# Three PSUM tiles, one load across two halves and a second store: a change to a batch-norm-ReLU kernel

## Chip, cores, metric

The kernel runs on one core of a Trainium2 chip. The metric is the device time of one execution in microseconds (us); lower is better.

## What is computed

```python
# x: (32, 128, 32, 32) float32; gamma, beta, running_mean, running_var: (128,)
normalized = (x - running_mean[None, :, None, None]) / np.sqrt(running_var[None, :, None, None] + eps)
scaled = normalized * gamma[None, :, None, None] + beta[None, :, None, None]
return np.maximum(scaled, 0).astype(np.float32)
```

With scale = gamma / sqrt(var + eps) and bias = beta - mean * scale, this is one ReLU(scale * x + bias) per row of 1024 numbers. 16.78 MB go in and 16.78 MB come out, and nothing is used twice.

## The kernel before

The 4096 rows (batch times channel) are laid out as two halves of 128 partitions x 16 rows. A partition's 16 rows lie next to each other in memory (64 KB), so a transfer of n rows is 128 runs of n x 4 KB. SyncE issues the loads, ScalarE runs the ReLUs in place and issues the stores, and a small chain of TensorE, ScalarE and VectorE makes scale and bias.

```python
TILES = ((0, 0, 2), (0, 2, 4), (0, 4, 8), (0, 8, 16), (1, 0, 16))   # half, first row, end

LOAD_CUTS = {(1, 8)}
STORE_CUTS = {(0, 1)}

HALVES = {(1, 0), (1, 1)}
# ... (cut: signature; P = 128, J = 16, HW = 1024, Q = 8)
    tiles = []
    for t, a, b in TILES:
        xt = data.tile([P, b - a, HW], F32, name=f"x{t}_{a}")
        cuts = [a] + [j for j in range(a + 1, b) if (t, j) in LOAD_CUTS] + [b]
        for c, d in zip(cuts, cuts[1:]):
            nc.sync.dma_start(out=xt[:, c - a : d - a, :], in_=xr[t, :, c:d, :])
        tiles.append((t, a, b, xt))

    raw = params.tile([Q, 4, J], F32, name="raw")
    for k, src in enumerate((running_var, gamma, running_mean, beta)):
        nc.scalar.dma_start(out=raw[:, k, :], in_=src.rearrange("(q j) -> q j", j=J))
    # ... (cut: eps_t, and rep, the 8 x 128 matrix that copies 8 partitions to 128)
    cols = psum.tile([P, 4, J], F32, name="cols")

    for a, b in ((0, 2), (2, 3), (3, 4)):
        nc.tensor.matmul(
            cols[:, a:b, :].rearrange("p k j -> p (k j)"),
            rep.rearrange("q r s -> q (r s)"),
            raw[:, a:b, :].rearrange("q k j -> q (k j)"),
            start=True,
            stop=True,
        )
    std_t = params.tile([P, J], F32, name="std_t")
    nc.scalar.activation(out=std_t, in_=cols[:, 0, :], func=ACTF.Sqrt, bias=eps_t[:, 0:1], scale=1.0)
    rstd_t = params.tile([P, J], F32, name="rstd_t")
    nc.vector.reciprocal(out=rstd_t, in_=std_t)
    scale_t = params.tile([P, J], F32, name="scale_t")
    nc.vector.tensor_mul(out=scale_t, in0=cols[:, 1, :], in1=rstd_t)
    ms_t = params.tile([P, J], F32, name="ms_t")
    nc.vector.tensor_mul(out=ms_t, in0=cols[:, 2, :], in1=scale_t)
    bias_t = params.tile([P, J], F32, name="bias_t")
    nc.vector.tensor_sub(out=bias_t, in0=cols[:, 3, :], in1=ms_t)

    with tc.manual_schedule(engines={mybir.EngineType.Activation}):
        for t, a, b, xt in tiles:
            first = a
            for j in range(a, b):
                step = HW // 2 if (t, j) in HALVES else HW
                for w in range(0, HW, step):
                    nc.scalar.activation(
                        out=xt[:, j - a, w : w + step],
                        in_=xt[:, j - a, w : w + step],
                        func=ACTF.Relu,
                        bias=bias_t[:, j : j + 1],
                        scale=scale_t[:, j : j + 1],
                    )
                if j + 1 == b or (t, j + 1) in STORE_CUTS:
                    nc.scalar.dma_start(
                        out=outr[t, :, first : j + 1, :], in_=xt[:, first - a : j + 1 - a, :]
                    )
                    first = j + 1
```

## Time and profile before

| what | value | from |
|---|---|---|
| time | 83.55 us, median of 3 (83.50 to 83.62) | timing |
| span of the profiled run | 81.7 us | page |
| ScalarE busy | 39.1 us, 48% | engine row |
| first load issued, first data packet | 0.81, 1.8 us | timeline, packet records |
| first ReLU, first store issued | 9.44, 10.71 us | timeline |
| last load landed, last store issued | 46.8, 55.95 us | timeline |
| DMA rate, 46.4 to 60.8 us | 435 GB/s | DMA view |

The lines behind this table stand in the prediction. In the timeline a line is: start, duration, engine (ACTq and SPq are the issuing sequencers of ScalarE and SyncE), source line, operation, and in brackets how long the engine was idle before and what ended that. In the DMA view each line of a queue gives packets, MB, and the time of its packets as a share of 16 engines' time. Three more lines are needed for comparison, the waits of the kernel before (in total, times, longest):

```profile
ACT x L105 <- DMA x<-in_x_dram: 7.7, 3, 3.6
...
ACT std_t L89 <- PE cols L81: 4.2, 1, 4.2
...
ACT x L105 <- DVE bias_t L97: 1.0, 1, 1.0
```

ScalarE waits for loads three times, 3.6 us at most; it waits for the last of the matmuls before its square root.

### The profile page before, as it was taken

Reading aid. Unit: us, or ns where it says so; the run is one execution under the profiler, and the core shown is the slowest. Engines: PE = TensorE matmul, PEld = TensorE weight load, DVE = VectorE, ACT = ScalarE, POOL = GpSimd, SP = SyncE. Lnnn points to the kernel's source line nnn. Section 1 sums busy time; section 2 is a strip of 40 time slices with the busy share of each in tenths; the row PEclk is TensorE's granted clock in tenths of the full one; section 3 lists DMA queues with packets and bytes.
Section 4 is the critical chain, followed back from the end, with each engine's and each line's share of the span. In section 5 each row is a group of like instructions: output and inputs, shape, how many; then the busy total and the mean of one; then the engine's idle time right before and its main releaser. Section 6 shows DMA issues by size and latency. Waiting matters only on the chain.

```text
span 81.7 us, 128 instructions
## 1 busy us (share of the span) xinstructions
PE 1.7 (2%) x6; PEld 1.5 (2%) x6; DVE 0.8 (1%) x5; ACT 39.1 (48%) x36; POOL 0.8 (1%) x6
## 2 busy tenths in 40 slices
PE   0008000000000000000000000000000000000000
PEld 0007000000000000000000000000000000000000
DVE  0000300000000000000000000000000000000000
ACT  0600477799039999199997199993000000000000
POOL 3000000000000000000000000000000000000000
DMA  2899999989899898969789699996991999998290
GB/s 44 313 422 481 409 481 417 497 369 497 369 385 481 375 491 357 541 293 605 321 373 589 273 489 393 513 497 273 513 770 64 449 513 513 513 513 385 128 513 0
DMA packets 1793, 33.56 MB, mean 411 GB/s; under 512 B 257, under 2 KB 257, under 8 KB 513
## 3 DMA queue, kind: packets, MB, share of 16 engines
q1 hardware_dynamic: 864, 16.78, 48.6%
q10 hardware_dynamic: 928, 16.78, 47.8%
q14 instruction: 1, 0.00, 0.0%
HBM read 16.78 MB, written 16.78 MB: 411 GB/s over the span
## 4 chain that ended last, share of the span: by engine, by line
DMA 56%; ACT 10%; issue 2%; SPq 0%
DMA x<-in_x_dram 56%; ACT x L105 10%; SPq L56 0%
## 5 line engine op out<-in xcount | busy, mean ns | idle before, releaser
L105 ACT ACTIVATE x<-x,bias_t,scale_t 128x1024 f32<-128x1024 f32 (+1 forms) x34 | 37.5, 1178 | 10.0 <-DMA x<-in_x_dram 7.7
L89 ACT ACT_TABLE_LOAD x1 | 1.3, 1283 | 2.7 <-issue 2.7
L89 ACT ACTIVATE std_t<-cols,eps_t 128x16 f32<-128x16 f32 x1 | 0.3, 276 | 4.2 <-PE cols L81 4.2
L81 PE MATMUL cols<-raw,rep 8*128 8x16 f32 (+1 forms) x6 | 1.7, 384 | 6.4 <-DMA raw<-in_gamma_dram 6.3
L81 PEld LDWEIGHTS cols<-raw,rep 8*128 8x128 f32 x6 | 1.5, 307 | 6.5 <-issue 6.3
L68 POOL TENSOR_SCALAR_AFFINE_SELECT rep<-rep 8x128 f32<-8x128 f32 x1 | 0.4, 394 | 0.1
L91 DVE RECIPROCAL rstd_t<-std_t 128x16 f32<-128x16 f32 x1 | 0.3, 253 | 7.5 <-ACT std_t L89 7.5
L67 POOL MEMSET rep<- 8x128 f32 x1 | 0.2, 195 | 0.3 <-POOLq L133 0.3
L93 DVE TENSOR_TENSOR scale_t<-cols,rstd_t 128x16 f32<-128x16 f32 x1 | 0.2, 174 | 0.1
L95 DVE TENSOR_TENSOR ms_t<-cols,scale_t 128x16 f32<-128x16 f32 x1 | 0.2, 174 | 0.0
L97 DVE TENSOR_TENSOR bias_t<-cols,ms_t 128x16 f32<-128x16 f32 x1 | 0.2, 174 | 0.0
L133 POOL MEMSET const-bfloat16-1.0<- 128x1 bf16 x1 | 0.1, 108 | 0.0
L133 POOL MEMSET const-float32-0.0<- 128x1 f32 x1 | 0.1, 105 | 0.3 <-issue 0.3
L133 POOL MEMSET const-uint8-127<- 128x1 uint8 x1 | 0.1, 107 | 0.0
L133 POOL MEMSET const-float32-1.0<- 128x1 f32 x1 | 0.1, 105 | 0.0
L65 DVE MEMSET eps_t<- 128x1 f32 x1 | 0.1, 59 | 0.9 <-PEq L133 0.9
## 6 DMA issues: line engine op xcount, KB each, us to landing
x<-in_x_dram SPq DMA_DIRECT2D x3, 4096.0 KB, 38.6
out_dram<-x ACTq DMA_DIRECT2D x1, 4096.0 KB, 28.6
x<-in_x_dram SPq DMA_DIRECT2D x2, 1024.0 KB, 5.8
x<-in_x_dram SPq DMA_DIRECT2D x1, 2048.0 KB, 11.3
out_dram<-x ACTq DMA_DIRECT2D x1, 2048.0 KB
out_dram<-x ACTq DMA_DIRECT2D x2, 512.0 KB, 19.1
out_dram<-x ACTq DMA_DIRECT2D x1, 1024.0 KB
raw<-in_running_var_dram ACTq DMA_DIRECT2D x1, 0.5 KB
```

What stands on the lines that cost most here:

```text
L65: nc.vector.memset(eps_t, float(eps))
L67: nc.gpsimd.memset(rep, 1.0)
L68: nc.gpsimd.affine_select(out=rep, in_=rep, compare_op=mybir.AluOpType.is_equal, fill=0.0, base=0, pattern=[[0, P // Q], [-1, Q]], channel ...
L81: nc.tensor.matmul(cols[:, a:b, :].rearrange("p k j -> p (k j)"), rep.rearrange("q r s -> q (r s)"), raw[:, a:b, :].rearrange("q k j -> q ...
L89: nc.scalar.activation(out=std_t, in_=cols[:, 0, :], func=ACTF.Sqrt, bias=eps_t[:, 0:1], scale=1.0)
L91: nc.vector.reciprocal(out=rstd_t, in_=std_t)
L93: nc.vector.tensor_mul(out=scale_t, in0=cols[:, 1, :], in1=rstd_t)
L95: nc.vector.tensor_mul(out=ms_t, in0=cols[:, 2, :], in1=scale_t)
L97: nc.vector.tensor_sub(out=bias_t, in0=cols[:, 3, :], in1=ms_t)
L105: nc.scalar.activation(out=xt[:, j - a, w : w + step], in_=xt[:, j - a, w : w + step], func=ACTF.Relu, bias=bias_t[:, j : j + 1], scale=sc ...
L133: nc = _bacc.Bacc("TRN2", target_bir_lowering=False, num_devices=1)
```

## The change

It does three things. The parameters get three tiles in PSUM (the memory into which TensorE writes the matmuls' results) and in SBUF (the one that holds the tiles of x) in place of one (variance and gamma share the first), so that a reader need not wait for matmuls that it does not use. Rows 8 to 15 of the first half and 0 to 7 of the second come in one 8 MB transfer, with a hand-built access pattern that jumps from half to half in each partition. Rows 8 to 15 of the second half get a tile of their own, and so the second half goes out in two stores of 4 MB in place of one of 8 MB. One ReLU fewer is cut in two.

```diff
-TILES = ((0, 0, 2), (0, 2, 4), (0, 4, 8), (0, 8, 16), (1, 0, 16))
-LOAD_CUTS = {(1, 8)}
+TILES = (((0, 0, 2),), ((0, 2, 4),), ((0, 4, 8),), ((0, 8, 16), (1, 0, 8)), ((1, 8, 16),))
-HALVES = {(1, 0), (1, 1)}
+HALVES = {(1, 0)}
 ...
+            (t0, a, b), (t1, c, _) = pieces
+            pitch = ((t1 - t0) * P * J + c - a) * HW
+            nc.sync.dma_start(
+                out=xt,
+                in_=bass.AP(tensor=xr.tensor, offset=xr[t0, :, a:b, :].offset,
+                    ap=[[J * HW, P], [pitch, 2], [HW, b - a], [1, HW]]))
+        for i, (t, a, b) in enumerate(pieces):
+            tiles.append((t, a, b, xt[:, i]))
 ...
-    raw = params.tile([Q, 4, J], F32, name="raw")
+    for a, srcs in ((0, (running_var, gamma)), (2, (running_mean,)), (3, (beta,))):
+        raw[a] = params.tile([Q, len(srcs), J], F32, name=f"raw{a}")
 ...
-    cols = psum.tile([P, 4, J], F32, name="cols")
+    cols = []
     for a, b in ((0, 2), (2, 3), (3, 4)):
+        c = psum.tile([P, b - a, J], F32, name=f"cols{a}")
 ...
```

(Cut: the branch for single pieces and the readers of the three tiles, which follow from this. Some lines are joined.)

More of the change, by code (lines that the diff above doesn't have):

```diff
@@ L51 @@
     tiles = []
-    for t, a, b in TILES:
-        xt = data.tile([P, b - a, HW], F32, name=f"x{t}_{a}")
-        cuts = [a] + [j for j in range(a + 1, b) if (t, j) in LOAD_CUTS] + [b]
-        for c, d in zip(cuts, cuts[1:]):
-            nc.sync.dma_start(out=xt[:, c - a : d - a, :], in_=xr[t, :, c:d, :])
-        tiles.append((t, a, b, xt))
-    raw = params.tile([Q, 4, J], F32, name="raw")
-    for k, src in enumerate((running_var, gamma, running_mean, beta)):
-        nc.scalar.dma_start(out=raw[:, k, :], in_=src.rearrange("(q j) -> q j", j=J))
+    for pieces in TILES:
+        n = len(pieces)
+        rows = pieces[0][2] - pieces[0][1]
+        xt = data.tile([P, n, rows, HW], F32, name=f"x{pieces[0][0]}_{pieces[0][1]}")
+        if n == 1:
+            ((t, a, b),) = pieces
+            nc.sync.dma_start(out=xt[:, 0], in_=xr[t, :, a:b, :])
+        else:
+            (t0, a, b), (t1, c, _) = pieces
+            pitch = ((t1 - t0) * P * J + c - a) * HW
+            nc.sync.dma_start(
+                out=xt,
+                in_=bass.AP(
+                    tensor=xr.tensor,
+                    offset=xr[t0, :, a:b, :].offset,
+                    ap=[[J * HW, P], [pitch, 2], [HW, b - a], [1, HW]],
+                ),
+            )
+        for i, (t, a, b) in enumerate(pieces):
+            tiles.append((t, a, b, xt[:, i]))
+    raw = {}
+    for a, srcs in ((0, (running_var, gamma)), (2, (running_mean,)), (3, (beta,))):
+        raw[a] = params.tile([Q, len(srcs), J], F32, name=f"raw{a}")
+        for k, src in enumerate(srcs):
+            nc.scalar.dma_start(out=raw[a][:, k, :], in_=src.rearrange("(q j) -> q j", j=J))
     eps_t = params.tile([P, 1], F32, name="eps_t")
@@ L76 @@
     )
-    cols = psum.tile([P, 4, J], F32, name="cols")
+    cols = []
     for a, b in ((0, 2), (2, 3), (3, 4)):
+        c = psum.tile([P, b - a, J], F32, name=f"cols{a}")
         nc.tensor.matmul(
-            cols[:, a:b, :].rearrange("p k j -> p (k j)"),
+            c.rearrange("p k j -> p (k j)"),
             rep.rearrange("q r s -> q (r s)"),
-            raw[:, a:b, :].rearrange("q k j -> q (k j)"),
+            raw[a].rearrange("q k j -> q (k j)"),
             start=True,
@@ L87 @@
         )
+        cols.append(c)
     std_t = params.tile([P, J], F32, name="std_t")
-    nc.scalar.activation(out=std_t, in_=cols[:, 0, :], func=ACTF.Sqrt, bias=eps_t[:, 0:1], scale=1.0)
+    nc.scalar.activation(
+        out=std_t, in_=cols[0][:, 0, :], func=ACTF.Sqrt, bias=eps_t[:, 0:1], scale=1.0
+    )
     rstd_t = params.tile([P, J], F32, name="rstd_t")
@@ L92 @@
     scale_t = params.tile([P, J], F32, name="scale_t")
-    nc.vector.tensor_mul(out=scale_t, in0=cols[:, 1, :], in1=rstd_t)
+    nc.vector.tensor_mul(out=scale_t, in0=cols[0][:, 1, :], in1=rstd_t)
     ms_t = params.tile([P, J], F32, name="ms_t")
-    nc.vector.tensor_mul(out=ms_t, in0=cols[:, 2, :], in1=scale_t)
+    nc.vector.tensor_mul(out=ms_t, in0=cols[1][:, 0, :], in1=scale_t)
     bias_t = params.tile([P, J], F32, name="bias_t")
-    nc.vector.tensor_sub(out=bias_t, in0=cols[:, 3, :], in1=ms_t)
+    nc.vector.tensor_sub(out=bias_t, in0=cols[2][:, 0, :], in1=ms_t)
     with tc.manual_schedule(engines={mybir.EngineType.Activation}):
```

## The prediction

> **What bounds the kernel now.** I read the page first: the busy row of the engines, then the DMA lines, then the chain that ended last.
>
> ```profile
> span 81.7 us, 128 instructions
> PE 1.7 (2%) x6; PEld 1.5 (2%) x6; DVE 0.8 (1%) x5; ACT 39.1 (48%) x36; POOL 0.8 (1%) x6
> ...
> HBM read 16.78 MB, written 16.78 MB: 411 GB/s over the span
> ## 4 chain that ended last, share of the span: by engine, by line
> DMA 56%; ACT 10%; issue 2%; SPq 0%
> ```
>
> No compute engine is busy for more than 48% of the span, and the chain runs mostly through loads. The chain as printed stops with ScalarE at 55.9 us, though the span is 81.7, so its last third is no instruction at all: it must be the stores draining. I checked that with the DMA view over three stretches: loads alone with the parameters, loads mixed with stores, stores alone. The first line of each is its packet count and rate, the following ones its queues (q1 carries the loads, q10 the stores and parameters).
>
> ```profile
> DMA packets 456, 4.13 MB, mean 409 GB/s; under 512 B 80, under 2 KB 80, under 8 KB 80
> ...
> DMA packets 868, 14.71 MB, mean 429 GB/s; under 512 B 98, under 2 KB 98, under 8 KB 354
> ## 3 DMA queue, kind: packets, MB, share of 16 engines
> q1 hardware_dynamic: 448, 12.58, 85.5%
> q10 hardware_dynamic: 420, 2.13, 14.9%
> ...
> DMA packets 284, 6.26 MB, mean 435 GB/s; under 512 B 30, under 2 KB 30, under 8 KB 30
> ```
>
> These are 2 to 12.1 us, 12.1 to 46.4 us and 46.4 to 60.8 us. The rate never leaves 409 to 435 GB/s, and the shares of the two queues in the middle stretch add to 100.4%: all 16 DMA engines are full from about 2 us until the end. (The 40-slice row seems to show holes late in the span, slices of 64 GB/s. A packet is counted in the slice where it starts, and the last packets are 64 KB and 2.4 us long, so holes are only the beat between packet and slice; over whole packets the rate is 435.) In the packet records of the trace I also summed what each packet took: divided by 16, 78.98 us per DMA engine, against a first data packet at 1.8 us and last ends between 80.2 and 80.6 us. There is no idle time to win between those points.
>
> The timeline shows the other side, when ScalarE hands stores over:
>
> ```profile
> 23.84 9.16 ACT L105 ACTIVATE x<-x,bias_t,scale_t 128x1024 f32<-128x1024 f32 x8 [3.59 <-DMA x<-in_x_dram]
> 33.02 0.34 ACTq L113 DMA_DIRECT2D out_dram<-x  x1
> 34.78 9.71 ACT L105 ACTIVATE x<-x,bias_t,scale_t 128x512 f32<-128x512 f32 x10 [1.79 <-DMA x<-in_x_dram]
> 46.77 9.16 ACT L105 ACTIVATE x<-x,bias_t,scale_t 128x1024 f32<-128x1024 f32 x8 [2.27 <-DMA x<-in_x_dram]
> 55.95 0.34 ACTq L113 DMA_DIRECT2D out_dram<-x  x1
> ```
>
> By the packet records, the store queue reaches the 32 KB packets of the store issued at 33.0 only at 51.2 us and the last store's 64 KB packets at 60.9 us, 4.9 us after its issue. ScalarE is ahead of the queue; its waits cost nothing.
>
> **What the Trainium skill says.** "DMA: Bandwidth & Descriptors", section "Where 436 GB/s comes from", gives 435.2 GB/s as the ceiling of the 16 DMA engines; the trace agrees (435 in the store stretch). The same page, "Queues, rings and completion order", says that each DMA engine round-robins between queue rows packet by packet. The trace agrees: in the mixed stretch q1 and q10 move about as many packets (448 and 420) but 12.58 against 2.13 MB, because the first stores have packets of 4 and 8 KB and the loads 32 KB. "PSUM — Partial Sum Buffer", section "PSUM bank collisions raise a hardware error", says that two engines must not touch one bank and 32-partition quadrant at once, disjoint columns included, so a reader has to be held back from a bank still being written; the trace fits, as the square root needs only the first matmul's columns and yet starts at 8.15 us, 0.04 us after the last matmul's end at 8.11.
>
> **The change, part by part.**
>
> Three PSUM tiles. The six PE instructions (two per matmul, about 0.3 us each) run from 6.33 to 8.11 us; the three matmuls start as gamma, mean and beta land (semaphores complete at 6.2, 6.8 and 7.5). With its own tile, the square root can start after the first matmul, about 7.0 instead of 8.15. Then square root 0.28, reciprocal 0.25, product 0.17 with the gaps of before end near 7.9; the second product follows; the subtraction still needs the third matmul at 8.11 and ends near 8.4 instead of 9.40. The first ReLU starts near 8.55 instead of 9.44, and the first store goes out about 0.9 us earlier. During all of this the DMA engines are full with loads. An earlier store only moves which bytes go first: 0 us at the end. Splitting the raw tile adds and removes no transfer: 0 us.
>
> The merged load. Two 4 MB loads become one of 8 MB, and the former two-part load of the second half is no longer one tile. A partition's run in DRAM is 32 KB in each half, so I expect the same 384 packets of 32 KB at 1.213 us (the median of before) in the load queue and the same order by bytes. One completion packet per DMA engine less (0.009 us). What moves is the landing of rows 8 to 15 of the first half: from 23.84 to when both pieces are there, near 34.8. Counting ScalarE forward: eight rows 34.8 to 44.0; store issued 44.0. The eight rows of the second half, one of them still in two pieces of 0.80 us, take 44.4 to 54.0; store issued about 54.0. The last eight, there since about 46.7, take 54.4 to 63.6; last store issued near 63.6.
>
> Is the store queue ever empty? Loads end at 46.4 as before. Then the remaining stores run alone: the 2 MB one (8 packets of 0.611 us per engine) until 51.3; the three 4 MB ones, 8 x 1.213 = 9.7 us each, until 61.0, 70.7 and 80.4. They are needed at 51.3, 61.0 and 70.7 and issued at 44.0, 54.0 and 63.6. Each is 7 us early, against the 1.0 us from issue to first packet of the first load (0.81 to 1.8). So ScalarE idles eleven microseconds more in the middle and it is hidden.
>
> The second half stored in two. Per DMA engine 8 packets of 64 KB at 2.418 us (19.34) become 16 of 32 KB at 1.213 (19.41): +0.06 us, and one completion packet more, +0.01. One store instruction more (0.34 us) on a ScalarE with slack: 0. One ReLU that was cut in two is now whole (HALVES loses a row), about 0.37 us less on ScalarE: 0.
>
> Sum: 83.55 + 0.06 + 0.01 - 0.01 + 0 = 83.6 us.
>
> **The rivals.** (1) *ScalarE starves the stores*: the merged load delays 8 of 32 rows by 11 us. For it: ScalarE does 24 of its 32 rows after 34.8 us, and its last store leaves 7.7 us later (63.6 against 55.95). Against it: 7 us of slack by the count above. If the merged load landed only with the last load (46.7 us), ScalarE would finish its 24 rows near 75.5; the last store alone then needs 1.0 + 9.7 more and the stores end near 86, some 6 us later: about 89 us, 7% slower. (2) *Completion semaphores are reused*: in before, the fourth load waits on the variance load's semaphore, the fifth on the mean's, the sixth on another load's. If an early store drew the semaphore of the 8 MB load, ScalarE would stand still from about 11 to 35 us, and the 30 rows left, about 37 us with the gaps, would put the last store at 72 and the end of the stores near 83, 2.5 us later: about 86 us. Before gives stores only semaphores long free, and there are 16 transfers now as before (4 + 6 + 6, 4 + 5 + 7), so I give it 2%. (3) *The merged pattern is cut by rows*: packets of 4 KB. They take 0.159 us, so 8 MB would be 128 x 0.159 = 20.35 us per engine in place of 19.41: 84.5 us, 1.1% slower, still "same". The single loads have the same row structure and are not cut. (4) *Faster through an earlier start or end*: the first load's issue (0.81 us) and first packet (1.8 us) aren't touched; the end has the same wait for the last 4-byte packets. An idle gap for a gain over 2% (1.7 us) doesn't exist while every byte still has to move: 33.55 MB at 435 GB/s are already 77.1 us.
>
> **Range and chances.** The sum is within run-to-run spread (83.5 to 83.62) of before. For 8 in 10 I take 83.2 to 84.0: half a per cent for chip and session on both sides, with a little of rival (3) above. Slower by over 2% needs rivals (1) or (2), faster over 2% has no mechanism: 0.01 faster, 0.96 same, 0.03 slower.
>
> **What the profile after would show.** Right: DMA rate over the span again 409 to 412 GB/s, 435 in stretches of stores alone; square root near 7.0 us; first ReLU near 8.5; ReLUs of rows 8 to 15 of the first half waiting on the load until about 34.8 for over 10 us; the last store issued near 63.6; q10 with 144 more packets (128 of data, 16 of completion), q1 with 16 fewer. Wrong: a stretch after 46 us with a DMA rate under 400 over whole packets (starved), an idle time of ScalarE ended by something other than a load, or a thousand or more packets in the load queue.

## The result and the profile after

The changed kernel took 83.68 us (median of 6 runs, 83.54 to 83.88), the kernel before beside it 83.57 (6 runs). The ratio of fast runs is 1.0012, with a 95% interval of 0.9996 to 1.0028: the same. A ratio here is the mean time of one kernel's fast runs over that of the other's of the same rounds, so it is not quite the ratio of the medians. All ratios below are to the kernel before.

The page after, span, queues and chain:

```profile
span 81.9 us, 128 instructions
...
q1 hardware_dynamic: 848, 16.78, 48.5%
q10 hardware_dynamic: 1072, 16.78, 47.7%
HBM read 16.78 MB, written 16.78 MB: 410 GB/s over the span
## 4 chain that ended last, share of the span: by engine, by line
DMA 41%; ACT 33%; issue 1%; ACTq 1%
```

Bytes, rate and span are as before. The printed chain looks quite different, with 33% ScalarE in place of 10%. That is not a new bound: the chain follows back from the last ReLU, which releases the last store, and the 7 MB or so still in the store queue then (17 us at 435 GB/s) are no instruction. The run that leaves a store out, below, puts this to the test.

The timeline after, from the square root on:

```profile
6.68 0.27 ACT L108 ACTIVATE std_t<-cols,eps_t 128x16 f32<-128x16 f32 x1 [2.82 <-PE cols L99]
...
9.39 0.37 ACTq L134 DMA_DIRECT2D out_dram<-x  x1
...
34.74 9.16 ACT L126 ACTIVATE x<-x,bias_t,scale_t 128x1024 f32<-128x1024 f32 x8 [15.82 <-DMA x<-in_x_dram]
43.92 0.34 ACTq L134 DMA_DIRECT2D out_dram<-x  x1
44.31 9.44 ACT L126 ACTIVATE x<-x,bias_t,scale_t 128x512 f32<-128x512 f32 x9 [0.42 <-ACT x L126]
53.78 0.34 ACTq L134 DMA_DIRECT2D out_dram<-x  x1
54.16 9.16 ACT L126 ACTIVATE x<-x,bias_t,scale_t 128x1024 f32<-128x1024 f32 x8 [0.42 <-ACT x L126]
63.35 0.34 ACTq L134 DMA_DIRECT2D out_dram<-x  x1
```

The first ReLU (not shown) starts at 8.12 instead of 9.44. The first store leaves 1.3 us earlier, the last one 7.4 us later, and ScalarE stands still for 15.8 us in one piece. None of it reaches the end. The DMA view from 46.4 to 80 us of the kernel before and then of the one after shows why:

```profile
DMA packets 428, 14.65 MB, mean 436 GB/s; under 512 B 46, under 2 KB 46, under 8 KB 46
```

```profile
DMA packets 584, 14.71 MB, mean 438 GB/s; under 512 B 68, under 2 KB 68, under 8 KB 68
```

The stores drain at one rate and without a break in both. In the packet records of the kernel after, the packets of the last store begin at 70.8 us, in the moment in which those of the store before end, 7.5 us after it was issued.

For the small differences I use one more reading of these records. For each packet I take what the same size usually takes (median of the kernel before: 4 KB 0.159 us, 8 KB 0.309, 16 KB 0.611, 32 KB 1.213, 48 KB 1.815 from the one run with such packets, 64 KB 2.418; a completion packet, 4 bytes at the end of each transfer on each engine, 0.009), add these up and divide by 16: the **time by size**. What the packets took above that is the **surplus**. Both are per DMA engine. Before: 78.04 by size and 0.75 surplus. After: 78.11 and 0.78. One caution: part of the surplus lies in the first 3 us, where the kernels hardly differ, and this part is 0.56 before and 0.29 after; what comes later is 0.18 before and 0.49 after. So the two totals agree by chance.

### The profile page after: what moved, and what is told of

Its sections match the earlier page's. It is cut to its first block, busy times and chain, and to the rows that moved or that the text cites. A ratio compares the mean times of both kernels' runs of the same rounds, so it can differ in the third digit from the quotient of the medians.

```text
span 81.9 us, 128 instructions
## 1 busy us (share of the span) xinstructions
PE 1.7 (2%) x6; PEld 1.5 (2%) x6; DVE 0.8 (1%) x5; ACT 38.8 (47%) x35; POOL 0.8 (1%) x6
## 3 DMA queue, kind: packets, MB, share of 16 engines
q10 hardware_dynamic: 1072, 16.78, 47.7%
## 4 chain that ended last, share of the span: by engine, by line
DMA 41%; ACT 33%; issue 1%; ACTq 1%
DMA x<-in_x_dram 40%; ACT x L126 33%; DMA raw<-in_running_var_dram 2%; ACTq L134 1%
## 5 line engine op out<-in xcount | busy, mean ns | idle before, releaser
L126 ACT ACTIVATE x<-x,bias_t,scale_t 128x1024 f32<-128x1024 f32 (+1 forms) x33 | 37.2, 1201 | 19.1 <-DMA x<-in_x_dram 15.8
```

Source lines behind the costliest of these rows:

```text
L126: nc.scalar.activation(out=xt[:, j - a, w : w + step], in_=xt[:, j - a, w : w + step], func=ACTF.Relu, bias=bias_t[:, j : j + 1], scale=sc ...
```

## Experiments

My theory: from 1.8 us on all 16 DMA engines are full, so only bytes, packet count and holes in the store queue count; an earlier first store and ScalarE's waits count for nothing until a hole opens. First rival: the parts cancel, the earlier start gaining what the merged load loses. Second rival: ScalarE or its chain is the bound, as the printed chain suggests. Seven runs test these; the other five look into a smaller effect that the first ones brought up, and into the price of a packet.

### Each part alone

**Three tiles alone** (the kernel before, raw tile left whole):

```diff
-    cols = psum.tile([P, 4, J], F32, name="cols")
+    cols = []
     for a, b in ((0, 2), (2, 3), (3, 4)):
+        c = psum.tile([P, b - a, J], F32, name=f"cols{a}")
```

> The kernel before with three PSUM tiles and nothing else. Theory (the DMA engines are full from 1.8 us on): the square root starts about 1.2 us earlier than 8.15, the first store goes out 1 us earlier or more, and the time stays at 83.57 within 0.2. Rival (the parts of the change cancel: an earlier start gains about 1 us, something else loses it): 82.5.

Measured: 84.08 us, ratio 1.0072 (1.006 to 1.0085). Both theory and rival missed it: no gain, but a loss of 0.6 us. The square root and the first store did move as expected:

```profile
6.73 0.27 ACT L89 ACTIVATE std_t<-cols,eps_t 128x16 f32<-128x16 f32 x1 [2.85 <-PE cols L80]
...
9.58 0.38 ACTq L113 DMA_DIRECT2D out_dram<-x  x1
...
47.68 9.16 ACT L105 ACTIVATE x<-x,bias_t,scale_t 128x1024 f32<-128x1024 f32 x8 [3.00 <-DMA x<-in_x_dram]
```

The last load landed at 47.68 instead of 46.77, and the surplus is 1.25 us instead of 0.75. That accounts for 0.5 of the 0.6 us. More on it below.

**The store split alone**:

```diff
-STORE_CUTS = {(0, 1)}
+STORE_CUTS = {(0, 1), (1, 8)}
```

> The kernel before with the second half stored in two and nothing else. Theory: 8 packets of 64 KB per engine become 16 of 32 KB, +0.06 us, the first of the two stores leaves near 44.5 instead of 55.95 and changes nothing: 83.6 within 0.2. Rival (the parts cancel; an earlier store of 4 MB gains): 82.5 or less.

Measured: 83.83 us, ratio 1.0035 (1.0023 to 1.0048), a loss of 0.3 us, and just outside the range that I had expected. By size it is 78.12, the 0.07 or 0.08 expected; the surplus is 0.69, no more than before. So nearly 0.3 us stay without an explanation in the packet records. There is no gain from the earlier store, as the theory says.

**The merged load alone**, with one 8 MB store for the second half:

```diff
+    xb = data.tile([P, 3, 8, HW], F32, name="xb")
 ... (cut: the first three tiles stay; one load for xb[:, 0:2], which is rows 8-15 of half 0 and
 ...  0-7 of half 1, and one for xb[:, 2])
+    tiles.append((0, 8, 16, xb[:, 0]))
+    tiles.append((1, 0, 16, xb[:, 1:3].rearrange("p a r w -> p (a r) w")))
```

> The kernel before with the merged 8 MB load and nothing else: the second half is still one store of 8 MB, issued after its sixteenth row. Theory: that store is now issued near 63.5 us, the store queue is empty at 60.9, and with 1.0 us from issue to first packet the DMA engines stand still 3.5 us: 87.1 us, about 4% slower, with a hole in the DMA rate between 61 and 64.5. Rival (the merged load is free by itself, ScalarE's wait being hidden): 83.6.

Measured: 86.57 us, ratio 1.0358 (1.0341 to 1.0376). The timeline and the stretches around the last issue (last column GB/s, before it the DMA share):

```profile
63.23 0.34 ACTq L125 DMA_DIRECT2D out_dram<-xb  x1
```

```profile
60.00:62.00 2.00, 0.00 (x0) 0.00 (x0) 0.00 (x0) 2.00 (x3) 0.00 (x0) 1.00 0.57 246
62.00:64.00 2.00, 0.00 (x0) 0.00 (x0) 0.00 (x0) 1.20 (x2) 0.00 (x0) 1.00 0.00 0
```

Here is a real hole: by the records the queue is empty at 61.4 on average and the last store's packets begin at 64.1, 2.7 us later and 0.9 us after the issue. The theory holds, with 2.7 us in place of the 3.5 expected; the rival that the merged load is free by itself falls. **The merged load needs the second store**: with it the last piece to wait for is 4 MB and is needed 9.7 us later.

### How much ScalarE may be late

**Late parameters**, on the kernel after:

```diff
+    for _ in range(16):
+        nxt = params.tile([P, J], F32, name=f"bias_{_}")
+        nc.vector.tensor_copy(out=nxt, in_=bias_t)
+        bias_t = nxt
```

> The kernel after with 16 small VectorE copies chained behind the bias, about 4 us, so that the first ReLU starts near 12 us instead of 8.1. Theory: the engines have loads to move meanwhile and the eight rows that are there finish near 23 us, long before the merged load lands: 83.7 within 0.3. Rival (the start of the first store is on the path, and three tiles paid for what the merged load cost): about 87.5.

Measured: 84.18 us, ratio 1.0082 (1.0068 to 1.0096). The first store left at 12.84 instead of 9.39, and 3.45 us of delay became 0.5 us of time. The rival's 87.5 is out; but 0.5 is more than the 0.3 that I allowed. The surplus is 1.22 against 0.78, which is 0.44 of it; but half of that (0.22) lies in the first 3 us, before the copies begin. The first store leaves later here than in the merged load alone (12.84 against 10.54), and still no hole opens, so it is not the early start from the three tiles that saves the merged load.

**Slow rows**: the last eight ReLUs in four pieces each, before and after.

```diff
                 step = HW // 2 if (t, j) in HALVES else HW
+                if t == 1 and j >= 8:
+                    step = HW // 4
```

> The kernel before with each of the last eight ReLUs cut in four. Wholes take 1.145 us apiece in a row, halves about 0.71, so quarters about 0.49: 1.97 a row, 6.6 us more in all. Theory: the last store (8 MB) is issued at 62.5 instead of 55.95, the queue is empty at about 61, and with 1.0 us from issue to first packet 2.5 us are lost: 86.1. Rival (ScalarE's lateness is always hidden): 83.6.

> The kernel after with the same cut. Theory: the last store (4 MB) is issued at 70.0 instead of 63.35, the queue is empty at 70.6, and with 1.0 us from issue to first packet only 0.4 us is lost: 84.1; so the changed kernel, though its ScalarE ends later, bears more delay than the kernel before. Rival (the merged load has used up ScalarE's slack): more loss than in the kernel before, 86.5 or over.

Measured: 85.93 us, ratio 1.0282 (1.0262 to 1.0301), on the kernel before; 83.89 us, ratio to the kernel before 1.004 (1.0018 to 1.0062), on the kernel after. The last issues, before and then after:

```profile
46.87 15.82 ACT L107 ACTIVATE x<-x,bias_t,scale_t 128x256 f32<-128x256 f32 x32 [2.25 <-DMA x<-in_x_dram]
62.72 0.34 ACTq L115 DMA_DIRECT2D out_dram<-x  x1
```

```profile
54.26 15.82 ACT L128 ACTIVATE x<-x,bias_t,scale_t 128x256 f32<-128x256 f32 x32 [0.42 <-ACT x L128]
70.11 0.34 ACTq L136 DMA_DIRECT2D out_dram<-x  x1
```

The same 6.7 us more of ScalarE open a hole of 2.5 us in the kernel before (61.2 to 63.6 by the records) and of 0.1 us after (71.0 to 71.1). The changed kernel ends its ScalarE work later and yet bears more delay, since its last store is needed later. That is the one thing which the change gains, and it shows only where ScalarE is slower than it is.

**A store left out**, on the kernel after (result wrong):

```diff
+                if (t, a) == (0, 4):
+                    continue
                 if j + 1 == b or (t, j + 1) in STORE_CUTS:
```

> The kernel after without the 2 MB store of rows 4 to 7 of the first half (result wrong on purpose). Theory: 8 packets of 0.611 us per engine fall out of a queue that is never empty, and the end comes 4.9 us earlier: 78.8. Rival (ScalarE or a chain of waits sets the end, as the printed chain with its 33% of ScalarE suggests): little change, 82 or more.

Measured: 78.99 us, ratio to the kernel before 0.9454 (0.943 to 0.9478); 4.7 us less than the 83.68 of the kernel after, where the bytes alone make 4.9. ScalarE's last store was issued at 63.28 as in the kernel after, so the bound is neither ScalarE nor the printed chain. The page of this run, whose span is 76.9 us:

```profile
HBM read 16.78 MB, written 14.68 MB: 409 GB/s over the span
```

The rate over the span is 409 GB/s, where the kernel after has 410: time goes with bytes.

### Where the 0.6 us of the three tiles went

The time by size is the same in three tiles alone as before; the surplus differs, and apart from the first packets of the kernel (0.3 to 0.6 us in every run) it sits in load packets, mostly between 12 and 48 us. Store packets had less than 0.02 us per engine in all, except after a hole. How far does the surplus after the first 3 us scatter from one execution to the next? Two runs above share all instructions with the kernel before up to 44 us or later, and have 0.31 (the store split) and 0.33 (slow rows before) against its 0.18 in the load packets; slow rows after has 0.47 against 0.49. So a difference under 0.15 says nothing. Three tiles alone, with 0.77, stand clear of that. Most of it comes in short events, 0.16 at 34 us and 0.38 from 44 to 46 us, far behind the first store.

**Unmixed**: three tiles alone, the stores issued by SyncE, so that they queue behind the loads.

```diff
-                    nc.scalar.dma_start(out=outr[...], in_=...)
+                    nc.sync.dma_start(out=outr[...], in_=...)
```

> Open after the first runs: three tiles alone cost 0.6 us (84.08). Its packet records show the load packets longer than the same sizes alone by 1.25 us per engine in all, 0.75 in the kernel before, nearly all while stores run beside loads, none in stores alone. This run is that kernel with its stores issued on SyncE, behind the loads in the same queue, so that loads and stores never run together. Theory A (reads slowed by writes beside them, more or less by how they happen to interleave): the surplus after 3 us falls to 0.1 or less and the time to about 83.1. Theory B (the earlier start of ScalarE or the tiles themselves cost the 0.6): 84.0 again.

Measured: 84.56 us, ratio 1.0114 (1.009 to 1.0137). Theory A fell in this form. (The expectation also says that nearly all of the surplus comes while stores run beside loads; that leaves out the first 3 us, with 0.48 of the 1.25 and 0.56 of the 0.75.) While loads ran alone, from 3 to 36 us, the surplus was 0.02; but the last two load packets of each engine before the first store packets, from 38.7 us on, took 1.7 to 2.1 us in place of 1.213, 1.15 us of surplus in all. ScalarE had begun its ReLUs at 8.34 us, so ScalarE's work beside loads is not what lengthens them. The DMA view from 15 to 36 us and from 36 to 43 us:

```profile
DMA packets 304, 8.91 MB, mean 424 GB/s; under 512 B 32, under 2 KB 32, under 8 KB 32
...
DMA packets 135, 2.32 MB, mean 332 GB/s; under 512 B 16, under 2 KB 16, under 8 KB 71
```

The second stretch is the changeover. Packets count where they start, so 332 overstates the dip; the 1.15 us is the better number.

**Tiles delayed**: three tiles alone and six small copies behind the bias, so that the first store leaves when it did before.

```diff
+    for _ in range(6):
+        nxt = params.tile([P, J], F32, name=f"bias_{_}")
+        nc.vector.tensor_copy(out=nxt, in_=bias_t)
+        bias_t = nxt
```

> Three tiles alone cost 0.6 us, and putting the stores behind the loads did not bring it back (84.56; the surplus of the load packets went from the mixed stretch to the last two load packets before the stores). This run is three tiles with six small VectorE copies of 0.21 us chained behind the bias, so that the first store goes out near 10.8 as in the kernel before (10.7), not at 9.6. Theory A (only the moment matters, at which stores come in among the loads): surplus 0.75 us per engine as before, 83.55 within 0.2. Theory B (the tiles cost it in another way): 84.1.

Measured: 83.68 us, ratio 1.0017 (1.0004 to 1.003), surplus 0.92, first store at 10.88. Doing more work brings 0.4 of the 0.6 us back, and no run of the one (83.51 to 83.74) reaches a run of the other (83.97 to 84.22). So by its time theory A stands: it is for the larger part the moment at which stores come in among the loads, and at most 0.2 us are left for the tiles themselves. The records agree only in part: after the first 3 us the surplus is 0.50, between the 0.77 of three tiles alone and the 0.18 to 0.33 of the kernel before and its two near copies. Nor does the first store's moment say all: the merged load alone, without three tiles and with its first store at 10.54, has 0.65 in its load packets, and late parameters, with 12.84, has 0.72. The stretch of 12.1 to 48 us, in turn of the kernel before, three tiles alone, and tiles delayed, in DMA rate:

```profile
DMA packets 928, 15.47 MB, mean 431 GB/s; under 512 B 112, under 2 KB 112, under 8 KB 368
```

```profile
DMA packets 908, 15.14 MB, mean 422 GB/s; under 512 B 110, under 2 KB 110, under 8 KB 366
```

```profile
DMA packets 917, 15.29 MB, mean 426 GB/s; under 512 B 109, under 2 KB 109, under 8 KB 365
```

The order of the three is the order of their times.

**Fewer packets**: the kernel before with loads of 8 MB and stores of 4 MB, and a version of three tiles with loads of 4, 12, 8 and 8 rows and 8 MB stores behind the loads.

```diff
-TILES = ((0, 0, 2), (0, 2, 4), (0, 4, 8), (0, 8, 16), (1, 0, 16))
-LOAD_CUTS = {(1, 8)}
-STORE_CUTS = {(0, 1)}
-HALVES = {(1, 0), (1, 1)}
+TILES = ((0, 0, 16), (1, 0, 16))
+LOAD_CUTS = set()                # large_unmixed: {(0, 4), (1, 8)}
+STORE_CUTS = {(0, 8), (1, 8)}    # large_unmixed: set(), and stores on SyncE
+HALVES = set()
```

> The kernel before with two loads of 8 MB (64 KB packets) and four stores of 4 MB, stores issued by ScalarE. By packet count: 16 load packets and 32 store packets per engine in place of 96, and four completion packets fewer, at 0.009 us each: -0.45 us, 83.1 if the surplus stays near 0.75. Rival (the first store comes so late that the store queue is empty once the loads end): a hole in the DMA rate between 40 and 46 us and 84 or more.

> Three tiles, loads of 4, 12, 8 and 8 rows, each half stored by one transfer of 64 KB packets that SyncE issues behind the loads. By packet count -0.45 us. If the changeover from loads to stores costs 1.15 us as in the unmixed run before: 84.0. If that surplus is the stores' data being read ahead, it grows with the first store packet (64 KB instead of 4): 85 or more. If it was chance: 82.9.

Measured: 84.62 us, ratio 1.0137 (1.0117 to 1.0157), and 84.67, ratio 1.0148 (1.0132 to 1.0163). The gain in time by size is there (77.60 in both against 78.04) and is lost again: surplus 1.58 and 1.72. The first time misses the 83.1 expected (it falls where the rival put it, but for another reason), and the second fits none of its three forecasts. In both most of it is one event, about 1.0 and 1.27 us, in the load packets just ahead of the first stores (33.8 us and 38.7 us on). There was no hole in either. With 64 KB packets of stores behind it the event was not much longer than with 4 KB ones (1.27 against 1.15), so it does not grow with the first store packet.

**Small packets**: the kernel after, with 64 bytes of padding behind each row of the last tile, so that 4 MB go in and out by rows of 4 KB.

```diff
-        xt = data.tile([P, n, rows, HW], F32, ...)
+        pad = 16 if pieces[0] == (1, 8, 16) else 0
+        xt = data.tile([P, n, rows, HW + pad], F32, ...)
+        xt = xt[:, :, :, :HW]
```

> The kernel after with 64 bytes of padding behind each row of the last tile, so that its 4 MB go in and out in packets of 4 KB. Theory (each packet costs about 0.009 us beside its bytes): 64 packets of 0.159 us in place of 8 of 1.213, twice: +0.94 us per engine, 84.6, within 0.5 for the surplus. The load lands near 51 us, before ScalarE comes to it at 54.2. Rival (packets overlap and their number costs nothing): 83.7.

Measured: 96.19 us, ratio 1.1519 (1.1498 to 1.1539), 11.6 us off the expectation. By size and surplus it has only 81.07 us per engine; the rest is mostly a hole of 10.9 us (72.3 to 83.2 by the records). The timeline of ScalarE and the DMA view from 50 to 68 us:

```profile
55.04 0.34 ACTq L136 DMA_DIRECT2D out_dram<-x  x1
73.07 9.16 ACT L128 ACTIVATE x<-x,bias_t,scale_t 128x1024 f32<-128x1024 f32 x8 [18.06 <-DMA x<-in_x_dram]
```

```profile
DMA packets 451, 7.80 MB, mean 433 GB/s; under 512 B 16, under 2 KB 16, under 8 KB 241
## 3 DMA queue, kind: packets, MB, share of 16 engines
q10 hardware_dynamic: 226, 6.88, 88.5%
q1 hardware_dynamic: 225, 0.92, 12.4%
```

226 store packets against 225 load packets, but 6.88 MB against 0.92. The load, in packets of 4 KB, takes turns with stores of 32 KB and gets about an eighth of their bytes; it lands at 73 us in place of the 51 expected, ScalarE waits 18 us, and the DMA engines run dry for over 10 us. The price of packets as such (0.94 us by size, 79.05 against 78.11) is there, but what I had missed was their price in turns. (The surplus of 2.02 is large too; 1.07 of it comes at 31 to 34 us, and I have no explanation for it.)

### The books

| kernel | by size | surplus | of it in the first 3 us | hole | time of the profiled run |
|---|---|---|---|---|---|
| before | 78.04 | 0.75 | 0.56 | 0 | 83.44 |
| after | 78.11 | 0.78 | 0.29 | 0 | 83.64 |
| split_store_alone | 78.12 | 0.69 | 0.38 | 0 | 83.73 |
| tiles_alone | 78.04 | 1.25 | 0.48 | 0 | 84.06 |
| tiles_delayed | 78.04 | 0.92 | 0.41 | 0 | 83.67 |
| late_parameters | 78.11 | 1.22 | 0.51 | 0 | 84.08 |
| merged_alone | 78.03 | 1.11 | 0.37 | 2.7 | 86.73 |
| slow_rows_before | 78.04 | 0.84 | 0.42 | 2.5 | 85.99 |
| slow_rows_after | 78.11 | 1.06 | 0.52 | 0.1 | 84.06 |
| skip_a_store | 73.21 | 0.61 | 0.47 | 0 | 78.98 |
| tiles_unmixed | 78.04 | 1.55 | 0.38 | 0 | 84.60 |
| large_packets | 77.60 | 1.58 | 0.60 | 0 | 84.66 |
| large_unmixed | 77.60 | 1.72 | 0.42 | 0 | 84.50 |
| small_packets | 79.05 | 2.02 | 0.51 | 10.9 | 96.36 |

Time minus size, surplus and hole is 4.4 to 5.5 us in every row, and 4.6 to 4.9 in the first nine: the start (1.8), the end of the span after the last packet (1.2 before), what the timing has beyond the span (1.7), and how unequally the 16 engines end. So three terms tell these kernels' times to within half a microsecond or so. The kernel before has the shortest measured time of all with full bytes; no run beat it.

## Why the prediction was right

- **The DMA engines bound the kernel: shown.** A store left out takes its own 4.7 to 4.9 us with it while ScalarE's issues stay where they were.
- **The landing and the three store issues: right.** Predicted 34.8, then 44.0, 54.0 and 63.6; the trace has 34.74, 43.92, 53.78 and 63.35. The store queue reached the last one at 70.8 against 70.7. The merged load kept its 32 KB packets (848 and 1072 packets in the queues, exactly the numbers predicted), so rivals (2) and (3) did not come about.
- **The split store, +0.06 us: right by size** (78.04 to 78.11 for the whole change); alone it measured +0.3, of which the records explain only this.
- **Rival (1), starved stores, was the right one to fear.** The merged load by itself costs 3.6%, 2.7 of the 3.1 us through just that mechanism. It is the change's own second store that turns it off, by moving the moment of need from 61 to 70.8 us.
- **"An earlier store only moves which bytes go first: 0 us at the end" is the step that was off.** Three tiles alone cost 0.6 us, 0.5 of it as longer load packets in the mixed stretch. In the whole change, too, the profiled execution had more of this after the first 3 us (0.49 against 0.18 to 0.33 in the kernel before and its two near copies). Yet the time over six runs rose by 0.1 us only. The parts measured alone, +0.6, +0.3 and +3.1 us, don't add up to that; the hole explains the last one, and for the first two the total came out right partly by luck. The split of the raw tile was never run by itself. The square root came at 6.68 rather than 7.0 and the first ReLU at 8.12 rather than 8.55, mostly because the matmuls began 0.3 us earlier than in the kernel before (6.04 against 6.33), as gamma landed earlier. Whether the wait in the kernel before came from the shared bank, as the prediction reads it, or only from the shared tile, no run separates.
- **The 78.98 us per DMA engine** that the prediction summed up include 14 packets of another queue (q14), most of them from before the span; without these it is 78.79. The conclusion doesn't change.
- **Rival (3)'s 84.5 us was worked out wrongly**, by packet price alone. The small-packet run shows that cutting a load into rows beside stores of large packets would also have changed its turns. The merged load was not cut, so this did no harm.

What remains open: why load packets lengthen beside stores and just ahead of them. That the moment matters is shown by the times (tiles alone against tiles delayed); which moments are good is not. That it needs packets of both kinds in flight at once is disproved in the records' terms (the unmixed run has it in the last two load packets). The records have one duration per packet, reading and writing together, so I cannot tell which side waits. Nearly 0.3 us of the split store are also unexplained.

## What to carry to other kernels

Before estimating what a wait costs, ask when the full queue behind it would need the result: here 15.8 us of idle ScalarE cost nothing, and an empty store queue of 2.7 us made up most of a loss of 3.1 us. A load merged for fewer transfers lands later as a whole, so check the last store's moment of need and cut that store if it is close. Where loads and stores take turns by packet, the packet sizes set who gets the bytes, and a transfer with small packets on the path of the last store can cost far more than its packets do.

## What the Trainium skill lacked or had wrong

- "DMA: Bandwidth & Descriptors", section "Queues, rings and completion order": turns by packet are confirmed (225 against 226 packets), but the section does not say what follows for bytes; 4 KB load packets beside 32 KB store packets got 0.92 MB of 7.80. What the profile records as one packet is a whole contiguous run, up to 64 KB (2.418 us).
- The same page, "Latency and other measured facts", gives about 600 ns to the first byte for transfers issued by SyncE or ScalarE. With the DMA engines idle, the time from the start of the issue to the first data packet, as a mean over the engines, was 0.9 us twice (63.23 to 64.13 and 62.72 to 63.62 us). From the end of the issue, 0.34 us later, it was 0.56 us, so the page's figure fits if it counts from there, which it doesn't say.
- The same page, "Why small descriptors are slow (HBM only)", gives the fixed cost per packet in cycles only; a figure in time stands elsewhere on the page, about 10.5 ns per packet in a small transfer, but for transfers issued by GpSimd. For those issued by SyncE and ScalarE the packet records here put it at about 0.009 us (4 KB takes 0.159 us, 8 KB 0.309).
- No page has it: load packets lengthen beside stores or just ahead of them, by 0.1 to 1.3 us per engine in all after the first 3 us. Moving the first store from 9.58 to 10.88 us took 0.3 us of it away, though the same program scatters by 0.15.
